# A hybrid attention layer on one core: first shift and scale in four groups, on-chip ranges by planned times, new cost figures

## The chip, the core and the metric

The kernel runs on one core of a Trainium2 chip. The core has a matrix engine (PE, with its weight loads shown as PEld), a vector engine (DVE), an activation engine (ACT), a general engine (POOL), a queue that issues DMAs (SP) and 16 DMA engines. The metric is device time in microseconds (us) of one execution, lower is better.

## The reference, cut to what matters

One layer over 512 latent tokens and 128 context tokens of width 1024, all in f32. A condition vector (one for the latents, one for the context) gives six rows of shift, scale and gate. The input is normalised, scaled and shifted, and one projection `w_in` feeds two head groups: latent attention (8 heads) and gated linear attention (4 heads, queries `gq`, keys `gk`, in chunks of 64). Both meet in `w_out`; a SwiGLU block follows.

```python
mod = silu(cond) @ w_ada + b_ada                      # 1024 -> 6 * 1024
sh1, sc1, gt1, sh2, sc2, gt2 = split(mod, 6)
h = rmsnorm(x, norm_attn) * (1 + sc1) + sh1
q_lat, kv_lat, k_rope, gq, gk, gv, gf_low, gb_low, g_out = split_in(h @ w_in)
attn = attention(rmsnorm(q_lat) @ w_uq, rmsnorm(kv_lat) @ w_ukv, k_rope)
o = rmsnorm(gla(gq, gk, gv, gates)) * silu(g_out)     # both directions
x = x + gt1 * (concat(attn, o) @ w_out)
h2 = rmsnorm(x, norm_ffn) * (1 + sc2) + sh2
x = x + gt2 * ((silu(a) * g) @ w_ffn_out)             # a, g = split(h2 @ w_ffn_in)
```

## The kernel before, in words

Tokens are five tiles of 128, four of latents and one of context; the 1024 features are eight tiles of 128. A product of the large kind is three matmuls (L212, L213, L214): both factors are split into a high part (ACT, L219) and a rest (DVE, L220).

**Start.** `early` loads x, then `w_ada`'s columns for the first shift and scale. `ada_first` makes four feature tiles at a time: eight loads of 128x2x512 (512 KB, runs of 2 KB), 16 matmuls on 32 columns of PE each (L399), a copy to SBUF (L408), 4 matmuls that turn the result (L414), three small additions and multiplications (L421 to L423). The first group (tiles 0 to 3) stands ahead of everything; the second (tiles 4 to 7) is due at feature tile 2. `features(k)` then scales a feature tile and splits it (ACT L551, DVE L553 to L555), and `product(k)` multiplies it with 448 columns of `w_in` (N_FIRST), whose rows are loaded in L582.

**Heads of the gated group.** `gla_qk` makes queries and keys with PE (L714), 48 matmuls of 320 columns for each of four pieces, here called gq0, gq1, gk0, gk1. Each piece needs its own 512 KB of `w_in` (L227), split by L219 and L220; ACT writes the result to SBUF (L1000 for queries, L1002 for keys), a DMA of SP moves each 64-partition half to the other partitions (L1003, "the moves"), and DVE multiplies with the decay (L1006, "the decay product"). The scores of the linear attention (L1074) need all four pieces. Between them stand the query latents: DVE normalises them (L539), PE turns them (L910), DVE takes them to SBUF (L549) and splits them (L554, L555).

**The first gate.** `ada_gate` makes it on DVE: per 128x1024 row block of `w_ada` two multiply-adds (L502). PE adds up over the partitions (L512), DVE adds the bias (L519). Other rows of the modulation come from PE (L443; loads L439).

**Second norm.** For each token tile DVE adds the gated projection to x (L1367, L1368), ACT squares (L1419) and scales it (L1421), PE turns it (L1431), and the SwiGLU products follow (L1568, L1617).

**Order.** `Plan` costs each instruction (`cost`), adds lags between engines (AFTER, BEFORE), lists 16 schedules with random variations and keeps the shortest; `keep` fixes the order on each engine. `Space.alloc` gives each range of SBUF and PSUM: of the ranges that fit, the one released longest ago in the order of the program. A range that is given again makes its new user wait for the old one.

Of the kernel before, what the change touches and what calls it, by code (L numbers as in the profile page):

```python
# [53 lines left out]
WARM = 20, 1, 2, 0  # L54
EARLY_ADA = 2

# [7 lines left out]
class Mem:  # L64
    def __init__(self, space, off, n):
        self.space, self.off, self.n = space, off, n
        self.ap = space.view(off, n)

    def v(self, pattern, **sizes):
        return self.ap.rearrange(pattern, **sizes)  # L70
# [5 lines left out]
class Space:  # L76
# [3 lines left out]

    def __init__(self, unit):
        self.unit = unit
        self.tensors = []
        self.segs = []
        self.clock = 0
        self.little = None

    def add(self, tensor, n, front=0, back=0):
        base = self.tensors[-1][0] + self.tensors[-1][1] + self.unit if self.tensors else 0
        self.tensors.append([base, n, tensor, base + front, base + n - back])  # L90
        self.segs.append((base, n, 0))
        return len(self.tensors) - 1
# [6 lines left out]
    def sides(self, i, front, back=0):  # L99
        base, n = self.tensors[i][:2]  # L100
        self.tensors[i][3:] = [base + front, base + n - back]

# [18 lines left out]
    def alloc(self, n, keep=False, within=None):  # L121
# [9 lines left out]
        for i in range(len(self.segs)):  # L131
# [32 lines left out]
    def release(self, m):  # L164
        self.clock += 1
        size = -(-m.n // self.unit) * self.unit
        self.segs.append((m.off, size, self.clock))
        self.segs.sort()
# [19 lines left out]
class Kernel:  # L188
    def __init__(self, tc, nc, A, O, plain, rounded, psum, dram, dbg=None):
        self.tc, self.nc, self.A, self.O = tc, nc, A, O  # L190
        self.sb, self.rb, self.ps = Space(16), Space(16), Space(512)
        self.sb.add(plain, N_PLAIN, FRONT_PLAIN, BACK_PLAIN)
        self.sb.reserve(512)
        self.rb.add(rounded, N_ROUNDED, FRONT_ROUNDED)
        self.ps.add(psum, 8 * 512)
# [87 lines left out]
    def constants(self):  # L283
# [33 lines left out]
            self.ident.rearrange("p (h a c) -> p a c h", h=2, a=2)[:, :, 0:2], axis=AX.X, op=ALU.add,  # L317
        )
        self.act_set(SET_SILU)

# [58 lines left out]

    def ada_load(self, c, i, raw):  # L380

        rv = raw.v("p (h a n) -> p h a n", h=2, a=2)
        for h in range(2):
            src = self.A["w_ada"][P * (i + 4 * h) : P * (i + 4 * h) + P, : 2 * D].rearrange("p (a n) -> p a n", a=2)
            self.nc.sync.dma_start(rv[:, h], src[:, :, 512 * c : 512 * c + 512])

    def ada_first(self, c, raws):


        nc, vec, tt = self.nc, self.vec, self.nc.vector.tensor_tensor  # L390
        cv = self.cond.v("p (h k c) -> p h k c", h=2, c=32)
        pb = self.bank(1, FREE)
        for i, raw in enumerate(raws):
            rv = raw.v("p (h a n) -> p h a n", h=2, a=2)
            group = []
            for h in range(2):
                for a in range(2):
                    r = 64 * h + 32 * a
                    group.append(nc.tensor.matmul(  # L399
                        pb.ap[r : r + 32], cv[:, h, i], rv[:, h, a], start=i == 0, stop=i == 3,  # L400
                        tile_position=(0, r),
                    ).ins)
            self.glue(group)
            raw.free()
            if c == 0:
                self.warm(WARM[2])
        t = self.sb.alloc(512)
        nc.vector.tensor_copy(t.ap, pb.ap)  # L408
        pb.free()

        pb = self.bank(1, FREE)
        o = pb.ap[:, :16].rearrange("p (b a c) -> p b a c", b=4, a=2)
        for b in range(4):
            nc.tensor.matmul(o[:, b], t.ap[:, P * b : P * b + P], self.halves, start=True, stop=True)  # L414
        t.free()
        shift, scale, norm = (
            vec[:, v + 4 * c : v + 4 * c + 4].unsqueeze(2).broadcast_to([P, 4, 2])
            for v in (V_BADA, V_BADA + 8, V_NA)
        )
        dst = self.A1[:, 4 * c : 4 * c + 4]  # L420
        tt(dst, o[:, :, 1], scale, op=ALU.add)  # L421
        tt(dst, dst, norm, op=ALU.mult)
        tt(self.B1[:, 4 * c : 4 * c + 4], o[:, :, 0], shift, op=ALU.add)  # L423
        pb.free()
# [135 lines left out]
    def start(self):  # L560
# [8 lines left out]
        for t, x in enumerate(xs):  # L569
            nc.sync.dma_start(x.ap, self.x_in(t))  # L570
        ada, win = [[], []], []

        def load_ada(c, i):
            raw = sb.alloc(2 * D)
            self.ada_load(c, i, raw)
            ada[c].append(raw)

# [6 lines left out]

        for i in range(4):
            load_ada(0, i)
        for k in range(4):
            load(k)
        for i in range(EARLY_ADA):
            load_ada(1, i)  # L590
        junk = self.bank(2)
# [46 lines left out]

        self.ada_first(0, ada[0])
        self.warm(WARM[3])  # L640
        self.idle.free()
        features(0)
        for i in range(EARLY_ADA, 4):
            load_ada(1, i)
        for k in range(KD):
            if k + 4 < KD:
                load(k + 4)
            if k == 2:
                self.ada_first(1, ada[1])
# [897 lines left out]
    def use(self):  # L1547

        return self.ready.pop(0)
# [460 lines left out]
def cost(ins):  # L2010
# [22 lines left out]
    if e == "Activation":  # L2033
        more = len(ins.outs) - 1 + sum(np.prod([c for _, c in a.ap[1:]]) == 1 for a in shapes[len(ins.outs) + 1 :])
        return 52 + n / 1.2 + 43 * (not in_psum) + 95 * more
    fast = not in_psum and (
        kind == "InstTensorCopy" or kind == "InstTensorScalarPtr" and not ins.is_scalar_tensor_tensor
    )
    if kind == "InstReciprocal":
        return 60 + 6.3 * n  # L2040
    if e == "Pool" and n > 1:
        return 150 + n * 2.1
    return 68 + n * (0.52 if fast else 1.042) + 60 * scalars * (kind == "InstTensorScalarPtr")


class Plan:
# [4 lines left out]
    def __init__(self):  # L2051
        self.nodes = []

    def take(self, nc, glued):
# [3 lines left out]
        for ins in nc.cur_bb.bb.instructions:  # L2058
            names = {a.bass_ap.tensor.name.split("_")[0] for a in (*ins.outs, *ins.ins) if hasattr(a, "bass_ap")}
            c = cost(ins)  # L2060
            if engine(ins) == "PE" and cold > 0:
                c *= 2
                cold -= c
            self.nodes.append((ins.name, type(ins).__name__, engine(ins), c, names))

    def lay(self, order, before):
# [39 lines left out]
    def orders(self, nc):  # L2106
# [26 lines left out]
        for i, n in enumerate(self.nodes):  # L2133
            for name, info in nc.dependency_edges(n[0]):
                if name in at and node[at[name]] != node[i]:
                    j = at[name]
                    lag = 0
                    if info.class_ == mybir.DependencyClass.Sync:
# [3 lines left out]
                        else:  # L2142
                            lag = AGAIN.get(a, 0)
                    lag += finish[j] - begin[i]
                    k = node[i]
# [33 lines left out]
        start = best[1]  # L2179
        self.length, self.start = float(best[0]), start  # L2180
        lanes = {e: [] for e in AFTER}
# [23 lines left out]

def trace(nc, last, dbg=None):

# [3 lines left out]
    with tile.TileContext(nc) as tc:  # L2211
        with (
# [6 lines left out]
            psum = ps.tile([P, 8 * 512], F32, name="psum")  # L2219
            k = Kernel(tc, nc, A, O, plain, rounded, psum, dr, D_)  # L2220

            with tc.tile_pool(name="early", bufs=1, reuse_waits="tile") as early:
                ids = [k.sb.add(early.tile([P, N_SHARED], F32, name=f"early{i}"), N_SHARED) for i in range(SHARED)]
                k.early(ids)
                for i in ids:
                    k.sb.remove(i)
            with tc.tile_pool(name="late", bufs=1, reuse_waits="tile") as late:
                for i in range(SHARED):
                    k.rb.add(late.tile([P, N_SHARED], F32R, name=f"late{i}"), N_SHARED)
                k.late()  # L2230
            last(tc, nc, k.glued)


def program(nc, dbg=None):
    plan = Plan()
    trial = type(nc)("TRN2", target_bir_lowering=False, num_devices=1)
    trace(trial, lambda tc, nc, glued: plan.take(nc, glued), dbg)
    lanes = plan.orders(trial)
    trace(nc, lambda tc, nc, _: keep(tc, nc, lanes), dbg)

# [17 lines left out]
```

## Time and profile before

| what | us |
|---|---|
| median of 3 runs | 836.67 |
| lowest, highest | 834.84, 839.66 |
| the profiled execution | 836.55 |
| its span, first to last instruction | 834.8 |
| PE busy in the span | 800.6 (96%) |
| DVE busy | 603.7 (72%) |
| ACT busy | 403.3 (48%) |

1.75 us of the profiled execution lie outside the span. PE's mean granted clock is 0.98 of full speed. PE stood idle for 34.2 us in all; where, and what ended the waits, the views further down show. A busy share over the whole span says little, as the stages have different limits.

### The profile page before, as it was taken

The numbers are of one execution on the slowest core, as the hardware profiler recorded it, in microseconds if no ns is written. First come the engines' busy times: TensorE is split into PE (matmuls) and PEld (weight loads), VectorE is DVE, ScalarE is ACT, GpSimd is POOL, SyncE is SP. The second block draws the span as 40 slices with busy tenths as digits, with TensorE's granted clock in tenths as the row PEclk, the third lists the DMA queues.
The fourth block names the chain that finished last, engine by engine and source line by source line (L and its number), as shares of the span: only waits on it lengthen the run. The fifth ranks groups of instructions, "written<-read, shape, count | busy, mean of one in ns | idle before, by whom it ended". The sixth has DMA issues, their size and how long they took to land.

```text
span 834.8 us, 13004 instructions
## 1 busy us (share of the span) xinstructions
PE 800.6 (96%) x4839; PEld 707.8 (85%) x4839; DVE 603.7 (72%) x1181; ACT 403.3 (48%) x816; POOL 4.8 (1%) x15
## 2 busy tenths in 40 slices
PE   8899989899998999998999999999999999999996
PEld 6698968587888787886999988999879998899985
DVE  5598995597756575379899732787896865899666
ACT  6267434224655668238655533555313553145522
POOL 0000000000000000000000000000000000000000
PEclk9999989899999999999999999999999999999998
DMA  9971346504542343642144332334875444555312
GB/s 340 311 275 44 105 134 189 183 26 123 159 87 64 91 125 129 227 127 102 51 127 152 95 117 86 92 117 126 292 213 181 122 128 151 191 177 149 98 58 98
DMA packets 102264, 118.17 MB, mean 142 GB/s; under 512 B 15671, under 2 KB 70065, under 8 KB 102201
## 3 DMA queue, kind: packets, MB, share of 16 engines
q1 hardware_dynamic: 102201, 117.35, 45.2%
q8 instruction: 38, 0.62, 0.3%
q14 instruction: 25, 0.20, 0.1%
HBM read 96.96 MB, written 13.55 MB: 132 GB/s over the span
## 4 chain that ended last, share of the span: by engine, by line
PE 79%; DVE 9%; DMA 6%; ACT 3%; issue 2%; SPq 0%; ACTq 0%; DVEq 0%
PE psum L1617 31%; PE psum L212 10%; PE psum L213 10%; PE psum L214 10%; PE psum L891 3%; PE psum L1568 2%; PE psum L1243 2%; PE psum L1312 2%; PE psum L714 2%; DMA plain<-in_w_ada 1%; PE psum L1298 1%; DMA plain<-plain 1%; DMA early<-in_x_prompt 1%; DVE plain L502 1%; DVE rounded L220 1%
## 5 line engine op out<-in xcount | busy, mean ns | idle before, releaser
L1617 PE MATMUL psum<-rounded,late 128*128 128x320 f32 x1764 | 259.5, 309 | 0.0
L1617 PEld LDWEIGHTS psum<-rounded,late 128*128 128x128 f32 x1764 | 259.0, 188 | 0.2
L219 ACT CAST late<-plain 128x512 fp32r<-128x512 f32 (+3 forms) x205 | 125.8, 618 | 154.5 <-PE psum L214 86.3
L220 DVE TENSOR_TENSOR late<-plain,late 128x512 fp32r<-128x512 f32 (+3 forms) x205 | 138.7, 685 | 76.2 <-ACT late L219 68.9
L212 PE MATMUL psum<-rounded 128*128 128x512 f32 (+2 forms) x224 | 80.1, 377 | 2.6 <-DVE rounded L554 1.9
L212 PE MATMUL psum<-late,rounded 128*128 128x512 f32 (+1 forms) x213 | 82.4, 387 | 0.0
L214 PE MATMUL psum<-late,rounded 128*128 128x512 f32 (+1 forms) x213 | 82.3, 386 | 0.0
L213 PE MATMUL psum<-late,rounded 128*128 128x512 f32 (+1 forms) x213 | 82.3, 386 | 0.0
L213 PE MATMUL psum<-rounded 128*128 128x512 f32 (+2 forms) x224 | 81.5, 374 | 0.8 <-DVE rounded L220 0.8
L219 ACT CAST rounded<-plain 128x256 fp32r<-128x256 f32 (+5 forms) x93 | 52.0, 581 | 58.8 <-DMA plain<-in_w_in 25.1
L214 PE MATMUL psum<-rounded 128*128 128x512 f32 (+2 forms) x224 | 79.4, 372 | 0.0
L220 DVE TENSOR_TENSOR rounded<-plain,rounded 128x256 fp32r<-128x256 f32 (+5 forms) x93 | 57.9, 642 | 24.2 <-ACT rounded L219 23.7
L212 PEld LDWEIGHTS psum<-rounded 128*128 128x128 f32 x224 | 41.9, 191 | 10.9 <-DVE rounded L554 2.0
L1626 ACT COPY plain<-psum 128x320 f32<-128x320 f32 x63 | 27.0, 428 | 48.0 <-PE psum L1617 47.7
L214 PEld LDWEIGHTS psum<-rounded 128*128 128x128 f32 x224 | 42.1, 191 | 6.6 <-issue 0.8
L212 PEld LDWEIGHTS psum<-late,rounded 128*128 128x128 f32 x213 | 40.0, 188 | 8.8 <-issue 0.8
L213 PEld LDWEIGHTS psum<-rounded 128*128 128x128 f32 x224 | 42.1, 192 | 6.3 <-DVE rounded L220 1.1
L214 PEld LDWEIGHTS psum<-late,rounded 128*128 128x128 f32 x213 | 40.0, 188 | 8.3 <-DVE rounded L220 0.2
L213 PEld LDWEIGHTS psum<-late,rounded 128*128 128x128 f32 x213 | 40.0, 188 | 7.9
L1243 PE MATMUL psum<-rounded 96*128 96x320 f32 x192 | 37.1, 327 | 3.3 <-ACT plain L278 1.4
L1622 DVE TENSOR_TENSOR plain<-plain,psum 128x320 f32<-128x320 f32 x63 | 30.6, 486 | 13.2 <-PE psum L1617 9.8
L502 DVE SCALAR_TENSOR_TENSOR plain<-plain 128x1024 f32<-128x1024 f32 x28 | 34.7, 1279 | 1.0 <-DMA plain<-in_w_ada 0.9
(278 smaller groups left out, 1106.7 us busy)
## 6 DMA issues: line engine op xcount, KB each, us to landing
plain<-in_w_ffn_in SPq DMA_DIRECT2D x44, 512.0 KB, 4.9
plain<-in_w_ada SPq DMA_DIRECT2D x42, 512.0 KB, 5.3
plain<-in_w_ffn_out SPq DMA_DIRECT2D x44, 256.0 KB, 2.9
y<-plain SPq DMA_DIRECT2D x20, 256.0 KB, 2.7
plain<-y SPq DMA_DIRECT2D x20, 256.0 KB, 3.5
early<-in_w_in SPq DMA_DIRECT2D x7, 512.0 KB, 4.7
early<-in_w_ada SPq DMA_DIRECT2D x6, 512.0 KB, 8.0
plain<-in_w_in SPq DMA_DIRECT2D x5, 512.0 KB, 4.3
```

The lines of the kernel that those rows point to most:

```text
L212: mm(out, lh, rh, start=start, stop=False)
L213: mm(out, lh, rl, start=False, stop=False)
L214: mm(out, ll, rh, start=False, stop=stop)
L219: self.nc.scalar.copy(hi, src).ins,
L220: self.nc.vector.tensor_tensor(lo, src, hi.bitcast(F32), op=ALU.subtract).ins,
L502: nc.vector.scalar_tensor_tensor(m.ap, raw.ap, x, m.ap, op0=ALU.mult, op1=ALU.add)
L714: mm(out[:, j], w[:, a], act[:, b, n * j : n * j + n], start=start and i == 0, stop=stop and i == 2,)
L891: self.nc.tensor.matmul(out, w[:, a], act[:, b], start=start and i == 0, stop=stop and i == 2)
L1243: nc.tensor.matmul(pv[:, n], q[:, a * TS + P * t : a * TS + P * t + P], k[:, b * KEYS + 320 * n : b * KEYS + 320 * n + 320], start=i == 0, ...
L1617: nc.tensor.matmul(ps, wv[:, k, a], right[:, k, b], start=first and k == 0 and i == 0, stop=k == 3 and i == 2, skip_group_check=not first,)
L1622: add = lambda out, x: nc.vector.tensor_tensor(out, x, by_tile(ps), op=ALU.add)
L1626: nc.scalar.copy(s[x].ap, ps)
```

## The change

It has three parts.

1. **Groups of two feature tiles.** `GROUPS = 2, 2, 2, 2`: the first shift and scale come in four groups, each from eight loads of 128x2x256 (256 KB, runs of 1 KB), 8 matmuls (L420 now), a copy, 4 turning matmuls (L436 now, with a constant `quarters` that one added reduction makes) and three small operations. In all there are 32 matmuls of the first kind as before, 16 of the turning kind (8 before), 4 copies (2), 12 small operations (6) and 32 loads (16) of the same bytes. The loads of three groups stand between the first rows of `w_in`.
2. **Ranges by planned times.** `program` plans up to three times. From the second plan on, `alloc` knows from the plan before when a range's last user ends (its stamp) and when the new user begins (need), and takes the range with the least `max(stamp - need, 0)`.
3. **Cost figures.** What follows a DMA: 600 ns + 0.9 of its cost, 960 before; a DMA's cost per run; ACT on 64 or fewer partitions +120 ns; scans, shuffles, copies to the rounded type and reductions from PSUM.

```diff
-EARLY_ADA = 2
+GROUPS = 2, 2, 2, 2
+EARLY_ADA = 3
...
-            cost = (-start,) if keep == BACK else (start,) if keep else (self.aside(start, size), stamp, got - size)
+            elif self.use:
+                need = self.use[len(self.log)][0]
+                cost = self.aside(start, size), max(stamp - need + SPARE, 0), need - stamp if FIT else stamp, got - size
...
-        self.segs.append((m.off, size, self.clock))
+        self.segs.append((m.off, size, self.use[m.number][1] if self.use else self.clock))
...
+    def ada_load(self, k, g, i, raw):
+        n = P * g
         rv = raw.v("p (h a n) -> p h a n", h=2, a=2)
         for h in range(2):
+            row = P * (2 * i + h)
+            src = self.A["w_ada"][row : row + P, : 2 * D].rearrange("p (a n) -> p a n", a=2)
+            self.nc.sync.dma_start(rv[:, h], src[:, :, P * k : P * k + n])
...
+        for s in range(2):
             group = []
+            for j in range(4):
+                rv = raws[2 * s + j // 2].v("p (h n) -> p h n", h=2)
+                group.append(nc.tensor.matmul(
+                    pb.ap[32 * j : 32 * j + 32, :n], cv[:, s, j], rv[:, j % 2], start=s == 0, stop=s == 1,
+                    tile_position=(0, 32 * j),
+                ).ins)
...
+        for i in range(2 * g):
+            nc.tensor.matmul(o[:, i], t.ap[:, P * i : P * i + P], self.quarters, start=True, stop=True)
...
+        groups = [(sum(GROUPS[:i]), g) for i, g in enumerate(GROUPS)]
+        for k, g in groups[:EARLY_ADA]:
+            load_ada(k, g)
+            for i in range(k, k + g):
+                if i < 4:
+                    load(i)
...
-AFTER = {"PE": 200, "DVE": 130, "Activation": 130, "Pool": 130, "SP": 960}
+AFTER = {"PE": 200, "DVE": 130, "Activation": 130, "Pool": 130, "SP": 600}
+TAIL = 0.9
+ROUNDS = 3
+SPARE, FIT = 0, False
...
-        return n * out.ap[0][1] / run * (9.4 + 4 * run * 0.0368) / 16
+        return n * out.ap[0][1] / run * (10.2 + 4 * run * 0.0398) / 16
...
+    for _ in range(ROUNDS):
+        plan, trial = Plan(), new()
+        try:
+            spaces = trace(trial, lambda tc, nc, glued: plan.take(nc, glued), dbg, use)
+        except MemoryError:
+            break
+        lanes = plan.orders(trial)
+        if best is None or plan.length < best[0].length:
+            best = plan, lanes, use, trial
+        use = plan.use(spaces)
```

The changed kernel's lines stand 14 to 22 further down: L399, L414, L212, L502, L539, L549, L554, L555, L714, L910 and L1006 are now L420, L436, L226, L523, L560, L570, L575, L576, L736, L932 and L1028; L227, L512, L519, L523 and L1003 are now L241, L533, L540, L544 and L1025.

What the change moves, at three places. First PE at the start, from the last turned x tiles (L605, now L626; L377 and L396 are idle matmuls that `warm` puts in) to the first 448-wide products (L212, now L226). Before:

```order
L605 MATMUL psum<-plain,early_71 128x128 x12
L377 MATMUL psum<-plain 128x128 x3
L399 MATMUL psum<-early_72,plain 32x512 x4
L399 MATMUL psum<-plain 32x512 x12
L377 MATMUL psum<-plain 128x128 x4
L414 MATMUL psum<-plain,early_69 128x4 x4
L212 MATMUL psum<-rounded 128x448
L213 MATMUL psum<-rounded 128x448
```

Now:

```order
L626 MATMUL psum<-plain,early_71 128x128
L420 MATMUL psum<-early_72,plain 32x512 x4
L420 MATMUL psum<-plain 32x512 x4
L626 MATMUL psum<-plain,early_71 128x128 x7
L436 MATMUL psum<-plain,early_69 128x2 x4
L626 MATMUL psum<-plain,early_71 128x128 x4
L420 MATMUL psum<-plain 32x512 x4
L226 MATMUL psum<-rounded 128x448
L227 MATMUL psum<-rounded 128x448
```

The first group's 8 matmuls come ahead of the last turned x tiles, and half of the second group's (4 of 8) ahead of the first product.

Second, DVE around the query latents, from the last small operations of the gates (L1048, now L1070) on. Before, where all 14 multiply-adds of the first gate (L502) are already done:

```order
L1048 TENSOR_TENSOR plain<-plain 128x5 x3
L549 TENSOR_SCALAR early_69<-psum,plain 128x128
L1006 TENSOR_TENSOR plain<-plain,early_70 128x640
L1006 TENSOR_TENSOR plain<-plain,early_71 128x640
L549 TENSOR_SCALAR early_71<-psum,plain 128x512
L549 TENSOR_SCALAR early_71<-psum,plain 128x128
L554 CAST rounded<-early_69 128x640
L554 CAST rounded<-early_71 128x640
```

Now:

```order
L1070 TENSOR_TENSOR plain<-plain 128x5 x3
L1028 TENSOR_TENSOR plain<-plain,early_72 128x640 x2
L570 TENSOR_SCALAR early_72<-psum,plain 128x512
L570 TENSOR_SCALAR early_72<-psum,plain 128x128
L575 CAST rounded<-early_72 128x640
L576 TENSOR_TENSOR rounded<-early_72,rounded 128x640
L570 TENSOR_SCALAR early_72<-psum,plain 128x128
L570 TENSOR_SCALAR early_72<-psum,plain 128x512
L523 SCALAR_TENSOR_TENSOR plain<-plain 128x1024 x2
L234 TENSOR_TENSOR rounded<-early_72,rounded 128x8x128
L523 SCALAR_TENSOR_TENSOR plain<-plain 128x1024 x2
L1071 TENSOR_TENSOR early_69<-early_69,plain 128x640
```

The two decay products of gq0 (L1006, now L1028) stand ahead of all four copies of turned query latents (L549, now L570) instead of between them, and four multiply-adds (L523) stand behind these copies, around the split of gk0's weights (L234 to 128x8x128).

Third, SP's queue at the loads of gk0's and gk1's weights (128x8x128). Before:

```order
L1003 DMA plain<-plain 64x640 x2
L227 DMA early_70<-in_w_in 128x8x128
L227 DMA early_71<-in_w_in 128x8x128
L507 DMA early_70<-in_b_ada 64x1024
L1003 DMA plain<-plain 64x640 x2
L523 DMA rows_110<-early_72 1x512 x2
```

Now:

```order
L1025 DMA plain<-plain 64x640 x2
L241 DMA early_72<-in_w_in 128x8x128
L528 DMA early_72<-in_b_ada 64x1024
L851 DMA plain<-in_rope 128x2x512
L1025 DMA plain<-plain 64x640 x2
L544 DMA rows_111<-plain 1x512 x2
L544 DMA rows_111<-early_69 1x512 x2
L241 DMA early_70<-in_w_in 128x8x128
L241 DMA early_72<-in_w_in 128x2x512
```

Before, both loads stand next to each other. Now gk1's load (into early_70) stands behind the moves of gq1 and the four writes of the first gate's rows (L544), and it waits until the first decay product of gq1 (L1028 from early_70) has read that range.

## Rows read from the trace of the kernel before

**Rows 1.** The page, busy time of each engine.

```profile
PE 800.6 (96%) x4839; PEld 707.8 (85%) x4839; DVE 603.7 (72%) x1181; ACT 403.3 (48%) x816; POOL 4.8 (1%) x15
```

**Rows 2.** Windows: stretch, length, busy per engine, PEclk (granted clock), DMA share, GB/s.

```profile
4.00:20.00 16.00, 15.71 (x119) 12.49 (x118) 10.31 (x35) 11.39 (x26) 0.31 (x1) 1.00 1.04 395
25.00:30.00 5.00, 3.11 (x11) 2.72 (x11) 4.50 (x12) 3.86 (x6) 0.00 (x0) 0.73 1.02 336
40.00:45.00 5.00, 5.00 (x29) 4.68 (x29) 3.88 (x11) 3.57 (x7) 0.00 (x0) 1.00 0.78 209
110.00:116.00 6.00, 2.95 (x14) 1.59 (x13) 5.30 (x17) 5.04 (x20) 0.30 (x1) 1.00 0.32 97
116.00:124.00 8.00, 7.45 (x31) 5.78 (x30) 7.20 (x35) 1.28 (x3) 0.65 (x1) 0.57 0.26 62
240.00:310.00 70.00, 63.02 (x447) 53.74 (x446) 42.22 (x93) 45.22 (x100) 0.00 (x0) 0.98 0.37 89
400.00:820.00 420.00, 420.00 (x2533) 393.38 (x2532) 315.12 (x510) 190.45 (x364) 0.00 (x0) 1.00 0.44 135
```

**Rows 3.** PE's waits: total, times, longest.

```profile
PE psum L1074 <- DMA plain<-plain: 3.2, 1, 3.2
PE psum L512 <- ACT plain L278: 3.0, 1, 3.0
```

**Rows 4.** Timeline, PE, 22 to 28 us: start, length, line, shape, [idle before].

```profile
22.31 1.05 PE L399 MATMUL psum<-plain 128*32 128x512 f32 x4 [0.33 <-DMA plain<-in_w_ada]
...
24.29 1.02 PE L414 MATMUL psum<-plain,early 128*128 128x4 f32 x8
27.20 0.63 PE L212 MATMUL psum<-rounded 128*128 128x448 f32 x1 [1.89 <-DVE rounded L554]
```

**Rows 5.** The chain of waits in order of time: start, length, what.

```profile
10.56 11.71 DMA plain<-in_w_ada
35.18 3.57 PE psum L399 x32
...
135.77 4.67 DMA early<-in_w_in
143.05 4.19 DMA plain<-plain
148.90 4.93 DMA plain<-plain
...
385.30 2.42 DMA x<-plain
```

**Rows 6.** Timeline, PE's gated-head products (L714).

```profile
104.54 7.04 PE L714 MATMUL psum<-rounded 128*128 128x320 f32 x46
...
138.93 7.89 PE L714 MATMUL psum<-rounded 128*128 128x320 f32 x52
```

**Rows 7.** Timeline, DVE, 113 to 128 us.

```profile
113.11 2.48 DVE L502 SCALAR_TENSOR_TENSOR plain<-plain 128x1024 f32<-128x1024 f32 x2
...
121.83 1.55 DVE L1006 TENSOR_TENSOR plain<-plain,early 128x640 f32<-128x640 f32 x2
123.41 1.01 DVE L549 TENSOR_SCALAR early<-psum,plain 128x512 f32<-128x512 f32 x2
124.34 0.88 DVE L554 CAST rounded<-early 128x640 fp32r<-128x640 f32 x2
125.26 1.56 DVE L555 TENSOR_TENSOR rounded<-early,rounded 128x640 fp32r<-128x640 f32 x2
```

**Rows 8.** Timeline, ACT, 115 to 117 us.

```profile
115.69 1.40 ACT L1000 ACTIVATE plain<-psum 64x640 f32<-64x640 f32 x2
```

**Rows 9.** Line L1003, the moves of 64 partitions.

```profile
DMA to landing us min/median/max: 2.5/2.5/2.5
```

**Rows 10.** Timeline, PE, 385 to 393 us.

```profile
389.14 0.39 PE L214 MATMUL psum<-rounded 128*128 128x512 f32 x1
391.95 1.41 PE L1431 MATMUL psum<-plain 128*128 128x128 f32 x8 [2.42 <-ACT plain L1421]
```

More of the change, by code (lines that the diff above doesn't have):

```diff
@@ L100, in sides @@
         base, n = self.tensors[i][:2]
[L101 removed]
+        self.tensors[i][3:5] = [base + front, base + n - back]
     def remove(self, i):
@@ L570, in start, with load_ada @@
             nc.sync.dma_start(x.ap, self.x_in(t))
[L571 to L576, printed above, removed]
+        ada, win = {}, []
+        def load_ada(k, g):
+            ada[k] = g, [sb.alloc(4 * P * g) for _ in range(4)]
+            for i, raw in enumerate(ada[k][1]):
+                self.ada_load(k, g, i, raw)
         def load(k):
@@ L642, in start @@
         features(0)
-        for i in range(EARLY_ADA, 4):
-            load_ada(1, i)
+        later = groups[EARLY_ADA:]
         for k in range(KD):
@@ L2034, in cost @@
         more = len(ins.outs) - 1 + sum(np.prod([c for _, c in a.ap[1:]]) == 1 for a in shapes[len(ins.outs) + 1 :])
-        return 52 + n / 1.2 + 43 * (not in_psum) + 95 * more
+        return 52 + n / 1.2 + 43 * (not in_psum) + 95 * more + 120 * (out.ap[0][1] <= 64 and n > 128)
     fast = not in_psum and (
@@ L2040, in cost @@
         return 60 + 6.3 * n
+    if getattr(ins, "is_tensor_tensor_scan", False):
+        return 68 + n * 2.22
+    if "Shuffle" in kind:
+        return 68 + n * 1.36
+    if kind == "InstTensorCopy" and fast and "float32r" in str(out.dtype):
+        return 68 + n * 0.71
+    if "Reduce" in kind and in_psum and n > 512:
+        return 68 + n * 1.042 + 120
     if e == "Pool" and n > 1:
@@ L2043, in cost, with columns @@
     return 68 + n * (0.52 if fast else 1.042) + 60 * scalars * (kind == "InstTensorScalarPtr")
+def columns(a):
+    tensor = a.bass_ap.tensor
+    lo = int(a.bass_ap.offset) % int(tensor.shape[-1])
+    return tensor.name.split("_")[0], lo, lo + 1 + sum(int(s) * (int(n) - 1) for s, n in a.ap[1:])
 class Plan:
     def __init__(self):
-        self.nodes = []
+        self.nodes, self.touched = [], []
     def take(self, nc, glued):
@@ L2064, in take, with use @@
             self.nodes.append((ins.name, type(ins).__name__, engine(ins), c, names))
+            self.touched.append([columns(a) for a in (*ins.outs, *ins.ins) if hasattr(a, "bass_ap")])
+    def use(self, spaces):
+        by = {}
+        for i, touched in enumerate(self.touched):
+            for name, lo, hi in touched:
+                by.setdefault(name, []).append((i, lo, hi))
+        out = []
+        for space in spaces:
+            times = []
+            for m in space.log:
+                base, tensor = space.of(m.off)[0], space.of(m.off)[5]
+                lo, hi = m.off - base, m.off - base + m.n
+                mine = by.get(tensor, [])
+                a = bisect.bisect_left(mine, (m.begin,))
+                b = len(mine) if m.end is None else bisect.bisect_left(mine, (m.end,))
+                ids = [i for i, x, y in mine[a:b] if x < hi and y > lo]
+                nodes = {self.node[i] for i in ids}
+                times.append((
+                    min((self.start[k] for k in nodes), default=0.0),
+                    max((self.start[k] + self.cost[k] for k in nodes), default=0.0),
+                ))
+            out.append(times)
+        return out
     def lay(self, order, before):
@@ L2179, in orders @@
         start = best[1]
-        self.length, self.start = float(best[0]), start
+        self.length, self.start, self.node = float(best[0]), start, node
         lanes = {e: [] for e in AFTER}
@@ L2228, in trace, with planned @@
                 for i in range(SHARED):
-                    k.rb.add(late.tile([P, N_SHARED], F32R, name=f"late{i}"), N_SHARED)
+                    k.rb.add(late.tile([P, N_SHARED], F32R, name=f"late{i}"), N_SHARED, name=f"late{i}")
                 k.late()
             last(tc, nc, k.glued)
-def program(nc, dbg=None):
[L2235 to L2239, printed above, removed]
+    return k.sb, k.rb, k.ps
+def planned(new, dbg=None):
+    best, use = None, None
+    for _ in range(ROUNDS):
[8 more added lines that the diff above has]
+        use = plan.use(spaces)
+    return best
+def program(nc, dbg=None):
+    _, lanes, use, _ = planned(lambda: type(nc)("TRN2", target_bir_lowering=False, num_devices=1), dbg)
+    trace(nc, lambda tc, nc, _: keep(tc, nc, lanes), dbg, use)
 def kernel(**inputs):
```

93 lines of the change are left out of this document (46 added, 47 removed).

## The prediction

> **What bounds the kernel now.** I read the busy times first, then the windows, PE's waits, and last the chain and the timelines at the places where the windows show a gap. PE is busy for 800.6 us of the span [rows 1], so a change that adds no speed to a matmul can win only the 34.2 us in which PE stands still and what a low clock costs beside them. In the windows [rows 2] the reader is to see where these lie: from 400 to 820 us PE is busy for all 420 us at clock 1.00, and nothing in this change touches that half. What is left are the start (3.11 of 5 us busy and clock 0.73 from 25 to 30 us), the wait for the query latents (2.95 of 6 us from 110 us, then clock 0.57 until 124), the moves before the linear attention's scores, the attention stage (63.02 of 70 us from 240), and the second norm. PE's waits [rows 3, 10] name what ended them: a DMA between partitions at L1074, ACT at L512 (its operand comes from DVE's gate sums, 2.48 us for the last two [rows 7], and PE's queue behind it holds the turning of the latents), ACT at L1431.
>
> A measurement of this kernel can tell about 0.5% from no change, here 4.2 us: 832.4 and 840.7. The sum is made against the profiled execution, 836.55, which stands 0.12 below the median of the runs.
>
> **The start.** The first 448-wide product begins at 27.20 [rows 4]. The chain [rows 5] shows why: the last load of the first group lands at 10.56 + 11.71 = 22.27, PE multiplies it at 22.31, and from there the copy, the turning (1.02), the scaling and the split take 27.20 - 22.31 = 4.89 us, which the change leaves as they are. The first group is now 2.10 MB in place of 4.19. From 4 to 20 us 395 GB/s arrived [rows 2], so the 2.10 MB that are left out take 5.3 us, and I put the first product at 21.9: **-5.3**. No row shows loads with runs of 1 KB by themselves. The slowest nearby row in which the loads of several sizes are mixed is 40 to 45 us, 209 GB/s at a DMA share of 0.78, or 268 GB/s of busy engines. At that rate the group takes 7.8 us after 10.56 and lands at 18.4, a gain of 3.9; at 395 it takes 5.3 and lands at 15.9, a gain of 6.4. I take 5.3, as the loads that it displaces ran in the same full queue.
>
> The Trainium skill, page "DMA: Bandwidth & Descriptors", section "Measured (HBM→SBUF, 128 partitions, SWDGE, issued from GpSimd)", speaks against the change: "Batch DMAs to ≥1 MiB for ≥75% of peak", with 138 GB/s at 64 KB and 341 at 1 MB. It would put 256 KB, halfway between them, at an estimated 240 GB/s, and the group at 10.56 + 8.75 = 19.3, a gain of 3.0. The trace does not agree for 512 KB, which reached 395 GB/s with several in flight [rows 2]; for 256 KB it is a rival below.
>
> What was ahead of the start now partly stands behind it. The second group took 3.57 us for four sets of four matmuls [rows 5], 0.89 a set. Before, four sets lay behind the first product; now six are left and the order puts one of them ahead of it, where PE waits anyway: one more, +0.9. Three turnings in place of one lie behind it, 1.02 each [rows 4]: +2.0. PE is busy without a gap there (5.00 of 5 us from 40), so both count: +2.9. The net of the start is **-2.4**; with the bounds of the rate it is -3.5 to -1.0. On DVE there are two more copies and six small operations, at most 0.5 us each by the copies of 512 columns and less (1.01 for two [rows 7]), some 4 us; DVE idles 1.12 of 5 us there [rows 2], which hides them over the 30 us of this stage; uncovered they would cost those 4. SP issues sixteen more DMAs of the same bytes; while the DMA engines are full (share 1.04) that costs nothing, and if it does, it shows as a lower rate, which the rival prices.
>
> **From the query latents to the last keys.** Before, gq0 ended at 104.54 + 7.04 = 111.58 [rows 6] and PE then waited 3.0 us. Four multiply-adds, two times 2.48 us [rows 7], are now behind the latents' copies, so what PE waited for comes some 5 us earlier on DVE, and the latents are ready when PE comes. But the order puts a new wait behind them: the two decay products of gq0 stand ahead of the four copies, and they need gq0's moves. I follow this chain, 2.4 us earlier. gq0 ends at 109.2; ACT's two writes take 1.40 [rows 8], a move 2.5 [rows 9], a decay product 0.8 (1.55 for two), so DVE is free at 113.9; four copies and one split take 2 × 1.01 + 0.44 + 0.78 = 3.2 [rows 7], and gq1 starts at 117.1. Its 48 matmuls take 7.04 × 48 / 46 = 7.35, to 124.5. The second chain is that of gk1's weights: their load now waits for gq1's decay product, 0.7 + 2.5 + 0.8 after gq1's end, so 128.5, lands 4.67 later [rows 5], is split by 134.3 (an estimated 1.1 for ACT's part, from its 0.7 for 640 columns [rows 8]), and gk1 ends at 141.7. PE has gk0 and the sums between them to do, 7.35 us and some 2, so it is not idle long. Before, gk1 ended at 138.93 + 7.89 = 146.82 [rows 6]: a gain of 5.1. PE still waits between 109.2 + 2.7 or so and 117.1 in two pieces, and after the same kind of gap its granted clock was 0.57 over 8 us, of which 7.45 were busy [rows 2]: 3.2 us lost. It would make the gain 1.9. Nothing excludes either; I take the middle, 3.6, that is **-1.2** beyond the start.
>
> After gk1 the moves decide. Before, the second write to SBUF waited for the decay product of the pair before it, which came after 143.05 + 4.19, and its own move ran from 148.90 for 4.93 [rows 5]; with 0.8 for the product that is 7.8 us after gk1's end. Now both writes wait for PE alone: 1.40 + 4.93 + 0.8 = 7.1, **-0.7** (0 if SP's queue holds the move as long, -3.1 if it takes 2.5).
>
> **Second norm.** PE's last main matmul starts at 389.14 and L1431 waits until 391.95 [rows 10]. The square of that tile began at 385.30 + 2.42 [rows 5], because its range overlapped the one of the tile before, which PE had yet to turn. The new ranges do not overlap for this tile, but now do for the next one. So 2.4 can go, or come back one tile later; I take **-1.0**.
>
> Everything else (lags and ranges of the attention stage, the SwiGLU products, the tail) I cost at nothing: hidden there by PE's queue, which is full from 400 us.
>
> Sum: -2.4 - 1.2 - 0.7 - 1.0 = -5.3, from 836.55 to **831.2**. Counted as the forecast is what ends between 828 and 832.4; by the bounds above it could end higher, which the first two rivals hold.
>
> **Rivals.**
> *Given back (834.6).* The start holds, but the low clock after the new wait costs its full 3.2: gk1 ends only 1.9 us earlier than before, and neither the moves nor the second norm add to it: 836.55 - 1.9 = 834.6. For it: the wait of 3.0 at L512 was followed by clock 0.57 [rows 2, 3]. Against it: the new gap is in two parts.
> *The start is bound by transfers (834.2).* At 268 GB/s the first group lands at 18.4; the order holds the first product behind half of the second group, 1.05 MB, with two rows of `w_in` (128 x 448 f32 each), 0.46 MB: 5.6 us more, 24.0, and 0.9 for the set, 24.9. That is -2.3, with the 2.9 behind it +0.6 in place of -2.4: 831.2 + 3.0 = 834.2. For it: runs half as long. Against it: 395 GB/s with the queue full.
> *Slower (842).* The moves take what they took beside loads, 4.93 and 4.19 in place of 2.5. Then DVE is free at 116.3, gq1 starts at 119.5 and with the low clock ends at 130.1, its decay product at 135.8, gk1's weights are split at 141.6, PE is idle before them and again at the low clock: gk1 ends at 141.6 + 7.35 + 3.2 = 152.1, 5.3 later than before: 841.9. It decides from the point at which gk1's weights come later than 139.5. For it: DVE and SP work in order, so each late move holds what stands behind it. Against it: the DMA share is 0.26 from 116 to 124 [rows 2].
> *More (827.7).* In the attention stage 7.0 of 70 us are idle [rows 2]; with lags that follow the trace half of it may go: 831.2 - 3.5. Nothing in the order shows it.
> *The change does not do what it says*, if the plan with the old ranges was the one kept. The order speaks against it: gk0's and gk1's weights lie in other ranges. I give it nothing.
>
> **How the numbers follow.** The forecast 0.40, given back 0.20, bound by transfers 0.12, slower 0.14, more 0.14. Faster by over 0.5% are the forecast and "more": 0.54. Within 0.5% are the second and the third: 0.32. Slower: 0.14. The range goes from 824, as "more" with the start's best bound, to 841, where the slower case begins to decide; about 0.05 lies below and 0.12 above.
>
> **What would show it.** The first 448-wide product at about 22 us (transfers: near 25). PE's 110 to 124 us: no wait at L512, but one at L910 or L714 for DVE's copies behind a decay product. The load of gk1's weights issued near 128.5 and L714's last piece ended near 142 to 145; at 150 the slower case holds. The wait at L1074 still some 3 us. The prediction is wrong if these places move as said and the time does not, that is, if another stage gives it back; the attention stage is the first to look at.

## The result, and the profile after

Median of five runs 828.15 us (825.1 to 830.87), the kernel before beside it 836.67: ratio 0.9896, 95% interval 0.9855 to 0.9936. The forecast was 831.2. The profiled execution took 828.15, with a span of 826.4 against 834.8, 8.4 less.

The windows of the changed kernel, same columns as [rows 2]:

```profile
4.00:20.00 16.00, 15.96 (x126) 13.68 (x125) 11.43 (x40) 12.24 (x28) 0.00 (x0) 1.00 1.06 384
20.00:25.00 5.00, 4.60 (x31) 2.82 (x23) 4.32 (x9) 2.16 (x4) 2.38 (x6) 1.00 1.00 332
25.00:30.00 5.00, 5.00 (x30) 4.30 (x27) 3.71 (x11) 1.99 (x3) 0.00 (x0) 1.00 1.00 333
110.00:116.00 6.00, 2.40 (x11) 2.16 (x12) 5.76 (x9) 1.07 (x2) 0.00 (x0) 0.82 0.36 87
116.00:124.00 8.00, 7.96 (x48) 6.86 (x46) 6.30 (x7) 0.96 (x2) 2.20 (x2) 0.92 0.32 98
240.00:310.00 70.00, 64.72 (x460) 54.41 (x459) 43.95 (x95) 45.69 (x101) 0.00 (x0) 0.98 0.38 101
```

PE is busy for 5.00 of 5 us from 25 us and its clock is 1.00 from 20 on, where before 3.11 of 5 us at 0.73 stood [rows 2]. The gap at the query latents is still there (PE busy for 2.40 of 6 us from 110 us), and the clock behind it is higher (0.92 from 116 to 124 us, 0.57 before). In the window from 240 to 310 us, in the attention stage, PE is idle for 5.3 us instead of 7.0.

PE's timeline at the start (PEld is the weight load in front of a matmul):

```profile
15.86 0.26 PEld L420 LDWEIGHTS psum<-plain 128*32 128x32 f32 x5 [0.17 <-DMA plain<-in_w_ada]
...
20.94 0.47 PE L226 MATMUL psum<-rounded 128*128 128x448 f32 x1 [0.40 <-DVE rounded L575]
```

The last wait for the first group's loads ends at 15.86, and the first 448-wide product starts at 20.94, 6.3 us earlier than in [rows 4]. From 4 to 20 us 384 GB/s arrived, with runs of 1 KB among the loads, against 395 with 2 KB.

The new work of this kind, grouped by line and shape, from the first 448-wide product to the first L714 product (L736 now): first before (27.2 to 103.5 us), then after (20.94 to 98). Columns: busy time, mean ns | idle before.

```profile
L399 PE MATMUL psum<-plain 128*32 128x512 f32 x16 | 1.9, 598 | 0.0
L399 PE MATMUL psum<-early,plain 128*32 128x512 f32 x16 | 1.9, 592 | 0.0
L414 PE MATMUL psum<-plain 128*128 128x4 f32 x8 | 1.1, 245 | 0.0
```

```profile
L420 PE MATMUL psum<-plain 128*32 128x512 f32 x24 | 3.0, 600 | 0.0
...
L436 PE MATMUL psum<-plain,early 128*128 128x2 f32 x16 | 2.1, 254 | 0.0
...
L420 PE MATMUL psum<-early,plain 128*32 128x512 f32 x16 | 1.9, 598 | 0.0
L436 PE MATMUL psum<-plain 128*128 128x2 f32 x8 | 1.0, 230 | 0.0
```

Behind the first product there are now 4.9 us of the first kind (3.8 before) and 3.1 us of the turning kind (1.1 before): 3.1 us more.

PE, DVE, SP and ACT from gq0 to gk1:

```profile
98.02 7.34 PE L736 MATMUL psum<-rounded 128*128 128x320 f32 x48
...
112.34 0.77 PE L932 MATMUL psum<-plain 128*128 128x128 f32 x5 [2.97 <-DVE early L570]
114.37 8.61 PE L736 MATMUL psum<-rounded 128*128 128x320 f32 x48 [1.27 <-DVE early L570]
...
134.65 7.89 PE L736 MATMUL psum<-rounded 128*128 128x320 f32 x52
...
109.84 1.55 DVE L1028 TENSOR_TENSOR plain<-plain,early 128x640 f32<-128x640 f32 x2
111.53 1.01 DVE L570 TENSOR_SCALAR early<-psum,plain 128x512 f32<-128x512 f32 x2
...
146.78 1.56 DVE L1028 TENSOR_TENSOR plain<-plain,early 128x640 f32<-128x640 f32 x2 [2.57 <-DMA plain<-plain]
...
96.46 0.38 SPq L241 DMA_DIRECT2D plain<-in_w_in  x1
...
127.37 2.44 SPq L241 DMA_DIRECT2D early<-in_w_in  x2
...
133.72 1.04 ACT L233 CAST rounded<-early 128x1024 fp32r<-128x1024 f32 x1 [1.01 <-DMA early<-in_w_in]
```

gq0 ends at 105.36; the decay products (L1028) run from 109.84, the copies (L570) only after them, and PE waits 2.97 and 1.27 us for the copies. gk1's load is issued at 127.37 and split from 133.72 on, and gk1 ends at 142.54, 4.3 us earlier than before [rows 6]. The last decay products end at 148.34.

PE and ACT at the second norm:

```profile
380.65 0.39 PE L228 MATMUL psum<-rounded 128*128 128x512 f32 x1
...
386.55 0.83 PE L1590 MATMUL psum<-rounded,late 128*128 128x256 f32 x2 [3.23 <-ACT rounded L233]
...
384.50 1.05 ACT L1441 ACTIVATE plain<-plain 128x1024 f32<-128x1024 f32 x1
...
386.10 0.70 ACT L233 CAST rounded<-plain 128x256 fp32r<-128x256 f32 x2
```

The wait of 2.4 at the turning [rows 10] is gone, and 3.23 us stand at the next product: the casts at 386.10 that it waits for are queued behind the square of the last tile (L1441), which itself started late.

### The profile page after: what moved, and what is told of

Read it like the earlier page. It is cut to its first block, busy times and chain, and to the rows that moved or that the text cites. A ratio compares the mean times of both kernels' runs of the same rounds, so it can differ in the third digit from the quotient of the medians.

```text
span 826.4 us, 13064 instructions
## 1 busy us (share of the span) xinstructions
PE 797.0 (96%) x4847; PEld 705.2 (85%) x4847; DVE 606.0 (73%) x1190; ACT 405.0 (49%) x816; POOL 5.8 (1%) x15
## 4 chain that ended last, share of the span: by engine, by line
PE 86%; DVE 9%; ACT 2%; issue 1%; DMA 1%; SPq 0%; DVEq 0%; ACTq 0%
PE psum L1639 31%; PE psum L226 11%; PE psum L228 11%; PE psum L227 11%; PE psum L913 3%; PE psum L736 3%; PE psum L1265 3%; PE psum L1590 2%; PE psum L1334 2%; PE psum L1320 2%; PE psum L396 1%; DVE plain L523 1%; PE psum L420 1%; PE psum L464 1%; DVE early L1064 1%
## 5 line engine op out<-in xcount | busy, mean ns | idle before, releaser
L234 DVE TENSOR_TENSOR late<-plain,late 128x512 fp32r<-128x512 f32 (+3 forms) x204 | 138.3, 686 | 71.1 <-ACT late L233 64.6
L227 PE MATMUL psum<-rounded 128*128 128x512 f32 (+2 forms) x230 | 82.5, 372 | 0.1
L226 PE MATMUL psum<-rounded 128*128 128x512 f32 (+2 forms) x230 | 80.1, 374 | 0.4 <-DVE rounded L575 0.4
L226 PE MATMUL psum<-late,rounded 128*128 128x512 f32 (+1 forms) x207 | 80.3, 388 | 0.0
L227 PE MATMUL psum<-late,rounded 128*128 128x512 f32 (+1 forms) x207 | 80.2, 387 | 0.0
L228 PE MATMUL psum<-late,rounded 128*128 128x512 f32 (+1 forms) x207 | 80.2, 387 | 0.0
L233 ACT CAST rounded<-plain 128x256 fp32r<-128x256 f32 (+5 forms) x91 | 50.0, 572 | 40.0 <-PE psum L228 14.6
L234 DVE TENSOR_TENSOR rounded<-plain,rounded 128x256 fp32r<-128x256 f32 (+5 forms) x91 | 55.7, 630 | 17.7 <-ACT rounded L233 17.2
L226 PEld LDWEIGHTS psum<-rounded 128*128 128x128 f32 x230 | 42.5, 190 | 9.6 <-ACT rounded L233 1.7
L228 PEld LDWEIGHTS psum<-rounded 128*128 128x128 f32 x230 | 42.8, 189 | 8.2 <-issue 2.5
L227 PEld LDWEIGHTS psum<-rounded 128*128 128x128 f32 x230 | 43.1, 190 | 6.3 <-DVE rounded L234 0.6
L226 PEld LDWEIGHTS psum<-late,rounded 128*128 128x128 f32 x207 | 38.9, 188 | 8.6 <-issue 0.8
L228 PEld LDWEIGHTS psum<-late,rounded 128*128 128x128 f32 x207 | 38.9, 188 | 8.2 <-DVE rounded L234 0.2
L227 PEld LDWEIGHTS psum<-late,rounded 128*128 128x128 f32 x207 | 38.9, 188 | 7.8
L1265 PE MATMUL psum<-rounded 96*128 96x320 f32 x192 | 39.1, 332 | 1.9 <-ACT plain L292 1.6
L1644 DVE TENSOR_TENSOR plain<-plain,psum 128x320 f32<-128x320 f32 x63 | 30.6, 486 | 11.9 <-PE psum L1639 9.9
L1265 PEld LDWEIGHTS psum<-rounded 96*128 96x128 f32 x192 | 29.9, 192 | 5.6 <-ACT plain L292 3.1
```

The source lines that it names most:

```text
L226: mm(out, lh, rh, start=start, stop=False)
L227: mm(out, lh, rl, start=False, stop=False)
L228: mm(out, ll, rh, start=False, stop=stop)
L233: self.nc.scalar.copy(hi, src).ins,
L234: self.nc.vector.tensor_tensor(lo, src, hi.bitcast(F32), op=ALU.subtract).ins,
L1265: nc.tensor.matmul(pv[:, n], q[:, a * TS + P * t : a * TS + P * t + P], k[:, b * KEYS + 320 * n : b * KEYS + 320 * n + 320], start=i == 0, ...
```

## Experiments

All ratios are to the kernel before, run beside each on the same chip.

| kernel | ratio (95%) | first 448-wide | last L714 | first L1568 | span |
|---|---|---|---|---|---|
| before | 1 | 27.20 | 146.5 | 394.9 | 834.8 |
| the change | 0.9896 (0.9855, 0.9936) | 20.94 | 142.2 | 386.5 | 826.4 |
| c1 groups only | 1.0184 (1.0146, 1.0222) | 23.02 | 167.5 | 408.7 | 848.9 |
| c2 ranges only | 0.9979 (0.9960, 0.9998) | 27.42 | 152.4 | 391.8 | 832.7 |
| c3 costs only | 0.9932 (0.9908, 0.9956) | 27.33 | 142.6 | 387.7 | 827.9 |
| c5 without ranges | 1.0259 (1.0226, 1.0292) | 21.88 | 167.3 | 416.9 | 856.8 |
| c6 without costs | 0.9970 (0.9952, 0.9988) | 21.52 | 145.1 | 392.1 | 832.6 |
| s1 the change, seed 1 | 1.0003 (0.9978, 1.0028) | 21.98 | 147.9 | 392.5 | 833.5 |
| s2 the change, seed 2 | 0.9986 (0.9962, 1.0010) | 21.25 | 147.2 | 391.3 | 831.5 |
| s3 before, seed 1 | 0.9983 (0.9962, 1.0005) | 27.28 | 143.9 | 389.6 | 829.5 |
| s4 costs only, seed 1 | 0.9954 (0.9933, 0.9975) | 27.78 | 143.6 | 393.2 | 832.2 |
| d1 start late | 0.9979 (0.9961, 0.9997) | 27.10 | 149.0 | 392.8 | 833.2 |
| f1 copies first | 0.9926 (0.9900, 0.9952) | 21.47 | 142.6 | 389.0 | 829.5 |
| f2 lateness first | 0.9891 (0.9869, 0.9914) | 22.50 | 145.3 | 384.4 | 825.3 |

The middle columns are starts in each profiled execution, in us: of the first 448-wide product, of the last matmul of gk1 (L714 of the kernel before, whatever its line there) and of the first L1568.

**The parts alone and taken away.** c1, c2 and c3 put one part into the kernel before, c5 and c6 take one out of the changed one:

```diff
-ROUNDS = 3
+ROUNDS = 1
```
(c5), and in c6 the old AFTER, DMA, ACT and DVE figures with TAIL = 0.

> The kernel before with the first part alone: groups of two feature tiles, old ranges, old cost figures. Theory A (the parts add up; the start belongs to the groups): first 448-wide product near 21 us as in the changed kernel, and about half of the 8.4 us of span, so a ratio of 0.994 to 0.996, some 832. Theory B (any new input makes the planner draw another list, and what lies behind the start is luck of the draw): the start comes at 21 us too, but the time lies anywhere from 826 to 838. Theory C (the gain needs the planned ranges): no better than 0.998, the earlier start is waited away by 160 us.

> The kernel before with the second part alone: ranges by planned times, the old groups and cost figures. Theory A: first product at 27.2 us as before, the waits of the attention stage (7.0 us idle from 240 to 310) fall by 2 to 3 us: ratio 0.996 to 0.998. Theory B: 0.988 to 1.005, without a pattern. Theory C: the largest part of the gain, 0.993 or less.

> The kernel before with the third part alone: the new cost figures, old groups and old ranges. (The changed kernel with the groups alone undone comes out as this same program, because the first of its plans is then kept.) Theory A: first product at 27.2, waits behind DMAs somewhat shorter, ratio 0.996 to 1.000. Theory B: 0.988 to 1.005. Theory C: 0.998 to 1.002.

> The changed kernel with the second part undone: one plan, ranges by age of release; groups and cost figures stay. Theory A: it keeps the start and loses 2 to 3 us in the attention stage: 0.992 to 0.994. Theory B: 0.985 to 1.000. Theory C: 0.998 or more, the attention stage idle for 7 us again.

> The changed kernel with the third part undone: old cost figures, groups of two and planned ranges stay. Theory A (the parts add up): 0.990 to 0.993, the start as in the changed kernel, a little more waiting behind DMAs. Theory B (luck of the draw): 0.985 to 1.000. Theory C (the ranges carry it): 0.988 to 0.992.

The parts do not add up, so theory A falls: 1.0184, 0.9979 and 0.9932 for the parts, 0.9896 together. Groups with the old ranges (c1, c5) are slower by 1.8 and 2.6%, though their first product comes 4 to 5 us earlier than before; neither A nor B had that. SP's queue, DVE and PE of c5 show why. Its timelines (L517 loads a row block of the first gate, L241 a piece's weights; each load below goes into the same range, early_72 from column 640):

```profile
66.90 12.52 SPq L517 DMA_DIRECT2D early<-in_w_ada  x3
...
117.05 0.34 SPq L517 DMA_DIRECT2D early<-in_w_ada  x1
...
123.31 0.38 SPq L241 DMA_DIRECT2D early<-in_w_in  x1
...
120.81 2.48 DVE L523 SCALAR_TENSOR_TENSOR plain<-early,plain 128x1024 f32<-128x1024 f32 x2 [1.11 <-DMA early<-in_w_ada]
...
128.29 1.44 PE L736 MATMUL psum<-rounded 128*128 128x320 f32 x4 [7.91 <-ACT rounded L233]
```

In that list, with ranges by age of release, all eight row blocks of the gate and the weights of gq0, gq1 and gk0 go through one range: a load, DVE's two multiply-adds (L523), the next load. gq1's weights could be loaded only at 123.31 and PE waited 7.91 us for them. c1 has the same single range, and PE waits 7.8 us there. In the changed kernel the row blocks and the weights of gq0 and gq1 have four ranges, and gq1's load was issued at 96.46. So the planned ranges are what makes the groups bearable, and theory C holds in this much: with them the groups come to 0.9970 in place of 1.0184 with the old cost figures (c6, c1), and to 0.9896 in place of 1.0259 with the new ones (the change, c5). That the ranges gain by themselves is not so (0.9979).

The cost figures alone give 0.9932, with the first product as late as before (27.33) and gk1's last matmul at 142.6, where the change has 142.2. As the changed kernel without its groups is this same program, the groups add 0.9896 against 0.9932, which the intervals do not separate; with the old figures they add nothing that can be measured (0.9970 in c6, 0.9979 in c2). So a gain of almost this size can be had without the early start.

**Luck of the draw.** `random.Random(0)` of the planner became `random.Random(1)` or `(2)`, in s1 and s2 of the changed kernel, in s3 of the kernel before, in s4 of c3.

> The changed kernel with another seed for the random variations of its 16 lists, nothing else. Theory A: 0.988 to 0.993, like the changed kernel's 0.9896. Theory B: a spread as wide as the effect, anywhere from 0.985 to 1.000, with the start unchanged and the difference behind it.

> As the run before, with a third seed. Theory A: 0.988 to 0.993. Theory B: 0.985 to 1.000.

> The kernel before with another seed for its lists. Theory A: 0.997 to 1.003. Theory B: 0.988 to 1.008, first product at 27.2 us in any case.

> The kernel before with the new cost figures alone, as c3_costs_only, but another seed for its lists. If the figures make better lists as such: 0.991 to 0.995, like c3_costs_only's 0.9932. Theory B: 0.988 to 1.005.

Theory B holds: the whole change with two other seeds is worth nothing that can be measured (1.0003, 0.9986), with about the same early start (21.98, 21.25). The table shows where the gain went: from the first 448-wide product to gk1's last matmul s1 and s2 take 125.9 and 126.0 us, the changed kernel 121.3, the kernel before 119.3. Another seed does not move the kernel before by anything that can be measured (0.9983). The cost figures did better than the kernel before with both seeds, by 0.7 and 0.5%, the second just outside the 0.991 to 0.995 that was expected; against the kernel before with that same seed (s3) it is 0.3%, which the intervals do not separate. Two or three seeds do not give the mean gain of any version. c1, c2, c5 and c6 have one seed each: the 1.8 and 2.6% of c1 and c5 are more than the 1.1% by which the seeds moved the change, the smaller differences may be the draw's.

**What the start is worth.** In d1 the first group's loads are issued twice; orders and ranges are those of the changed kernel.

```diff
+            if k == 0 and self.twice:
+                self.extra.append(self.nc.sync.dma_start(rv[:, h], src[:, :, P * k : P * k + n]).ins.name)
```

> The changed kernel with its orders and ranges as they are, but the eight loads of the first group issued twice, to the same place, so that the start comes later and nothing else changes its place. Asks what an early start is worth. The second loads wait for the first, so the first 448-wide product should come near 25 us in place of 20.94, some 4 us later. Theory D (the start is on the path): the whole delay is still there at the first product of gq0 (98.0 us in the changed kernel), at the end of gk1 (142.5) and at the end: 832, ratio 0.994. Theory E (DVE's list and its loads set when the keys are ready, and the start has slack): the delay is gone by the end of gk1, less than 1 us at the end, ratio 0.990.

PE of d1 (L227 is the first 448-wide product, L739 gq0 and gk1):

```profile
27.10 0.47 PE L227 MATMUL psum<-rounded 128*128 128x448 f32 x1
...
104.21 7.34 PE L739 MATMUL psum<-rounded 128*128 128x320 f32 x48
...
141.45 7.89 PE L739 MATMUL psum<-rounded 128*128 128x320 f32 x52
```

The start came 6.2 us later, more than meant. gq0 starts 6.2 later, gk1's last piece 6.8, the span is 6.8 longer. Theory D holds for this list: no slack between the first loads and the end took the delay up. It delays all loads behind the group too, so it does not say that PE alone is the bound.

**The new wait before gq1.** DVE's products stood ahead of the copies because the copies' buffer (1024 to 1664 of early_72) was given the place of a decay that the second product still had to read. f1 moves that buffer and then, on DVE, the two products:

```diff
+LO = 229
+MOVED = {146: 16032, 147: 16032}
...
+    row = lanes["DVE"]
+    row[LO : LO + 8] = row[LO + 2 : LO + 8] + row[LO : LO + 2]
```

> The changed kernel with two edits and nothing else: the latents' two buffers of 128x640 lie in a range that no decay uses, and on DVE the two decay products of gq0 stand behind the four copies of the turned latents in place of ahead of them. Theory F (as predicted: PE's new wait before gq1 comes from these products, which the shared range forces ahead): the waits of 3.0 at the turning and 1.3 at gq1 fall to under 2 us together, gq1 starts 1.5 to 2.5 us earlier than 114.4, gk1 ends 1 to 2.5 us earlier than 142.5, 826 to 827, ratio about 0.988. Rival G (the wait only changes its name: gk0's load now starts 3 us later, and DVE has the same work): gq1 starts earlier, gk1 ends at 142.5 or later, ratio 0.9896 or more.

PE of f1 (L941 the turning, L745 gq1, L542 the gate's sums):

```profile
111.16 0.77 PE L941 MATMUL psum<-plain 128*128 128x128 f32 x5 [1.28 <-DVE plain L579]
113.19 7.38 PE L745 MATMUL psum<-rounded 128*128 128x320 f32 x48 [1.27 <-DVE plain L579]
121.81 2.24 PE L542 MATMUL psum<-plain 128*32 128x512 f32 x4 [1.24 <-DVE plain L532]
...
125.24 1.05 PE L542 MATMUL psum<-plain 128*32 128x512 f32 x4 [0.84 <-DVE plain L549]
```

The first two waits fall from 4.2 to 2.55 (not under 2, as F had it), and gq1's matmuls take 7.38 us in place of 8.61. The 1.27 at gq1 stays: both buffers of the latents lie on one range, in f1 too (16032 twice in the edit), so the second pair of copies stands behind the split of the first (L575 and L576 in the changed kernel). f1 did not part them. But the gate's sums now wait 1.24 and 0.84 and run longer, and from the first product to gk1's last matmul it takes 121.1 us against 121.3. Rival G holds: gq1 starts earlier (113.19 for 114.37), gk1 ends at 142.95, DVE has the same work, and the wait moved. The time cannot be told from the changed kernel's.

**Lateness before preference.** In f2 the rule puts lateness first:

```diff
-                cost = self.aside(start, size), max(stamp - need + SPARE, 0), need - stamp if FIT else stamp, got - size
+                cost = max(stamp - need + SPARE, 0), self.aside(start, size), need - stamp if FIT else stamp, got - size
```

> The changed kernel with one line of its rule turned: lateness by the plan comes ahead of the preference for a part of SBUF (in the changed kernel the preference comes first, so a range that the plan itself gives as late is taken while others are free). This makes new plans. Theory F: the latents' buffers no longer share with the decays, fewer waits before gq1, 0.986 to 0.990. Theory B (a new list is a new draw): 0.985 to 1.002, and the waits go where that list puts them.

0.9891, the same as the change's 0.9896, with waits of 5.2 in all at the turning: not fewer before gq1, so theory F falls for it. Theory B holds: it is a new list, in which gk1 ends 3 us later and the stretch from there to the first L1568 is 5 us shorter (239.1 for 244.3), and no better version that can be measured.

## Why the prediction was right, point by point

The time lies in the range and on the side that was forecast, 3 us below the forecast itself. It is nearer to the rival "more" (827.7) than to the forecast (831.2). In the profiled executions the terms measure as follows, with the forecast in brackets: the start -3.8 (-2.4), on to gk1's end -0.5 (-1.2), from there to the first L891 -1.2 (the moves, -0.7), from there to the last main matmul -3.0 (nothing), the second norm +0.2 (-1.0), the rest -0.1, in all -8.4 (-5.3). The 5.5 us up to the first L891 came where 4.3 were forecast. That the start gave 1.4 more and the second norm 1.2 less than forecast nearly cancels, which is luck.

- **The start.** Forecast: group on the chip at 16.97, product at 21.9. Measured: 15.86 and 20.94. The bound at 395 GB/s (15.9) was the right one, and the 18.4 of the rival (at 268 GB/s) was not. Nor does the trace bear out the estimate of 19.3 that was worked out from the Trainium skill's table ("DMA: Bandwidth & Descriptors", section "Measured (HBM→SBUF, 128 partitions, SWDGE, issued from GpSimd)"): with loads of 256 KB from SP in the queue beside others, 384 GB/s arrived. The added work was +2.9 by the sum, +3.1 by the rows. Not in the sum: PE was busy for 4.60 of the 5 us from 20 on and its clock stayed at 1.00, where before it was 0.73 from 25 to 30. The last matmul of the projection (256 wide) starts at 97.90 for 104.42, 6.5 earlier; 12 matmuls of 512 columns, some 2.7 us, have moved behind gq0 by then. So -3.8 for -2.4.
- **To the last keys.** The chain came as worked out: decay products done at 111.39 (113.9), gq1 at 114.37 (117.1) and at a low clock at first (8.61 us for 7.35), its end 122.98 (124.5), gk1's load 127.37 (128.5), gk1's end 142.54 (141.7). PE no longer waits at the gate's sums (L533), as was said. The gain by there, 4.3, is between the two ends 1.9 and 5.1; 3.6 was taken. f1 shows that a part of PE's wait hangs on the shared range (4.2 to 2.55 us), and that gk1's end does not (142.95). That the gain would belong to one seed was not foreseen.
- **The moves.** 7.1 us after gk1's end were forecast for the last decay product; it ended 148.34 - 142.54 = 5.8 after it. Before it was 153.92 + 0.82 - 146.82 = 7.9, so this is -2.1, of which 1.2 are left at the first L891. PE's wait before the scores fell from 3.25 to 2.07, where the prediction had it stay.

```profile
153.67 0.86 PE L1074 MATMUL psum<-plain 64*128 64x128 f32 x4 [3.25 <-DMA plain<-plain]
...
153.92 0.82 DVE L1006 TENSOR_TENSOR plain<-plain,early 128x640 f32<-128x640 f32 x1 [0.31 <-DMA plain<-plain]
```

```profile
147.66 0.33 PE L1085 MATMUL psum<-plain 128*128 128x128 f32 x1 [2.07 <-DVE plain L1028]
```

- **The second norm** is the step that failed in sign. -1.0 was forecast; from the last main matmul's start to the first L1617 it was 401.04 - 389.14 = 11.9 and is 392.76 - 380.65 = 12.1. The wait came back one tile later, as the prediction allowed and did not take.
- **The attention stage** was costed at nothing, as hidden by PE's queue "which is full from 400 us". That reason does not reach the stage, which ends before 390 us, and this is where the missing 3 us are: from gk1's end to the last main matmul it was 389.14 - 146.82 = 242.3 us and is 380.65 - 142.54 = 238.1; 1.2 of the 4.2 lie ahead of the first L891. This is the rival "more" (from half of 7.0 us idle), to which 0.14 was given. Which part of the change shortens the stage is not shown: the stretch from the last L714 to the first L1568 in the table is 239 to 250 us over all lists, 248.4 before and 245.7 in s3, 244.3 in the change, 244.6 and 244.1 in s1 and s2, 245.1 and 249.6 with the cost figures alone.
- **The range.** Its lower end, 824, does not come out of the terms given for it: "more" with the start's best bound is 827.7 - 1.1 = 826.6. The time lies above both.

So the forecast's reason, an early start that a DVE chain partly takes back, was right for this list as far as gk1's end, which is 4.3 of the 8.4 us. The prediction was worked out from this one list, and the seeds show that its gain is not a worth of the three parts as such.

## What to carry to other kernels

Where a planner with random tries fixes the order, a change to it is measured with several seeds: here one seed gives 0.9896 and two others 1.0003 and 0.9986, and the table's stretches tell what stays over the seeds (the early start) from what belongs to a list. Before tiles of a load are cut smaller, look at which ranges their neighbours will be handed: the same cut came out 1.8 and 2.6% slower where eight loads and three pieces' weights fell into one buffer. A wait that is forced by a shared range can move on when the range is freed, if the engine behind it has as much to do as before, as in f1.

## What the runs showed of the hardware

About the same idle time is not always followed by a low clock. In f1 and in the changed kernel the attention stage has the same order, and PE is idle for about as long from 260 to 270 us; columns as in [rows 2], the changed kernel first, then f1:

```profile
260.00:270.00 10.00, 7.56 (x54) 6.40 (x53) 6.42 (x14) 4.68 (x12) 0.00 (x0) 1.00 0.56 153
270.00:280.00 10.00, 10.00 (x81) 7.53 (x81) 5.33 (x12) 6.85 (x16) 0.00 (x0) 1.00 0.16 36
```

```profile
260.00:270.00 10.00, 7.68 (x53) 6.43 (x51) 6.19 (x14) 4.24 (x11) 0.00 (x0) 0.90 0.58 153
270.00:280.00 10.00, 10.00 (x61) 6.74 (x62) 3.47 (x8) 5.42 (x12) 0.00 (x0) 0.75 0.08 17
```

In the changed kernel the clock stays at 1.00. In f1 it is 0.90 and then 0.75, so its profiled execution lost some 0.10 x 7.68 + 0.25 x 10.00 = 3.3 us there with the same work. A profiled execution alone does not settle 0.3%.

The executions of one program differ in the same way. The changed kernel's five took 825.1, 826.32, 828.15, 829.95 and 830.87 us at a mean granted clock of 0.992, 0.989, 0.988, 0.982 and 0.980. This is not all that sets the seeds apart: s1 took 835.3 to 836.0 us at 0.982, s2 833.2 to 833.5 at 0.980, and the kernel before 836.55 at 0.980. But a part of the 8.4 us between the two profiled executions goes with it: they ran at 0.980 and 0.988, and the changed kernel's run at 0.980 is 5.7 us shorter than the one before. Whether such a part is chance or comes from the list's own waits, no run here separates.
